# Layer 1 of a hybrid decoder: recurrence and output projection in one loop over blocks of 128 tokens

## The chip, the cores and the metric

The kernel runs on one core of a Trainium2 chip. The metric is the device time of one execution in microseconds, shown as the median of three runs. Beside it stands one execution with the hardware profiler on. Engines are named as the profile does: PE is TensorE's matrix unit and PEld its weight load, DVE is VectorE, ACT is ScalarE, POOL is GpSimd, SP issues most DMAs.

## The reference, cut to what matters

Two residual layers, 2048 tokens, width 1024, fp32. Layer 0 is a pooling and convolution mixer, layer 1 a gated DeltaNet with 8 heads of 128; each is followed by a mixture of experts. Layer 1's mixer is this:

```python
def gated_deltanet_mixer(h, w_in, conv_w, a_log, dt_bias, onorm_g, w_out):
    u = h @ w_in
    ...
    o = chunk_gated_delta_rule(l2norm(q), l2norm(k), v, beta, g)
    o = o * lax.rsqrt(jnp.mean(o * o, axis=-1, keepdims=True) + EPS) * onorm_g * jax.nn.silu(z)
    return o.reshape(bsz, seq, DN_WIDTH) @ w_out

# inside chunk_gated_delta_rule, for one chunk after the other:
def step(state, xs):
    qg_i, kd_i, u_i, w_i, a_i, d_i = xs
    v_new = u_i - jnp.einsum('bhck,bhkv->bhcv', w_i, state)
    o_i = jnp.einsum('bhck,bhkv->bhcv', qg_i, state) + jnp.einsum('bhcm,bhmv->bhcv', a_i, v_new)
    state = state * d_i[..., None, None] + jnp.einsum('bhck,bhcv->bhkv', kd_i, v_new)
    return state, o_i

# and around the mixer, in each layer:
    x = x + g_m * y
    hn = rmsnorm(x, norm_ffn[l]) * (1.0 + sc_f) + sh_f
    x = x + g_f * hierarchical_moe(hn, w_grp[l], b_grp[l], w_exp[l], b_exp[l], w_up[l], w_down[l])
```

What is left out of the mixer cuts u into q, k, v (after a short convolution and silu), z, beta and g.

## The kernel before

Layer 0 and its experts come first and are the same in both kernels. In layer 1, `dn_project` computes the projections of all tokens and stores what the recurrence needs to DRAM (`stg`, with A, KE, QG, KDD and VP for each block and head; `zT`; the diagonal blocks `ndia` for the inversion, and more).

`dn_chain` (from line 1320) then runs 16 blocks of 128 tokens in order, in two groups of four heads. `M(bl, hg)` assembles the block's inverse T out of 32x32 pieces: `spread` on POOL makes block-diagonal operands (`na`, `xo`, `tt`, line 1347), and six small steps alternate PE with DVE and ACT. `R(bl, hg)` is the recurrence: KE times the state S, `dv` on DVE (line 1454), T times dv (copied to `vt` by ACT), the output `po`, and the new state S (line 1472), for which POOL multiplies the old S by `etot` (`sd`, line 1459). `tail` makes the factor of the output norm (`ors` on POOL, `fac` on DVE) and scales the output on ACT; `O` transposes it on PE and multiplies it by onorm on DVE (line 1508) into a tile that is stored to `yT` in DRAM. The steps are generators, and the loop's body writes out by hand in which order their pieces are emitted; Tile's scheduler then gives each engine its own sequence, and an engine works through its sequence in order. Beside the first blocks, `dn_invert(1, 1)` inverts the diagonal blocks of the second half's second head group in 31 column steps on DVE (lines 1312 and 1313, tiles `xtmp` and `xblk`).

Then `out_phase(1, ...)` (from line 460) runs over the same 16 blocks. It loads w_out and splits it into a high and a low half (`woh`, `wol`; the helper `split`, lines 233 and 234, one on ACT, one on DVE); for each block it loads yT and zT, multiplies them (line 486), splits the product, and projects it with 48 matmuls of 128x512 (line 532: high by high, low by high, high by low). DVE multiplies the result by the gate row gm (line 536) and adds x (line 537); ACT takes the squares (line 540), `rstd` makes the norm's factor (`rs1t` on DVE, `rs` on POOL, lines 187 and 189), and DVE applies it and the shift (lines 542 and 543; in layer 0 line 543 is on POOL). The block goes to DRAM (`acc`, `hn`). `logits` transposes it and multiplies it by the routing weights, for two blocks at a time (line 567); `route` is called for groups of 4, 4, 4, 3 and 1 blocks, and `rank_experts` at the end. `moe(1)` follows.

## Time and profile before

| what | value |
| --- | --- |
| median of three runs | 3415.38 us (3412.9 to 3416.74) |
| the profiled execution, its own time | 3413.42 us |
| its span, from first to last instruction | 3411.7 us |
| PE busy | 2937.8 us, 86% |
| DVE busy | 2482.2 us, 73% |
| ACT busy | 1455.1 us, 43% |
| POOL busy | 1124.4 us, 33% |
| mean granted clock of PE | 0.927 |

The times of the profiled execution stand beside its own time, not beside the median. An engine's share is a mean over stages that have different limits, so the stages are read one by one. A wait is put down to the engine or DMA whose event came last. "Clock" is the share of full speed that the chip granted to PE in a stretch.

### The profile page before, as it was taken

Reading aid. Unit: us, or ns where it says so; the run is one execution under the profiler, and the core shown is the slowest. Engines: PE = TensorE matmul, PEld = TensorE weight load, DVE = VectorE, ACT = ScalarE, POOL = GpSimd, SP = SyncE. Lnnn points to the kernel's source line nnn. Section 1 sums busy time; section 2 is a strip of 40 time slices with the busy share of each in tenths; the row PEclk is TensorE's granted clock in tenths of the full one; section 3 lists DMA queues with packets and bytes.
Section 4 is the critical chain, followed back from the end, with each engine's and each line's share of the span. In section 5 each row is a group of like instructions: output and inputs, shape, how many; then the busy total and the mean of one; then the engine's idle time right before and its main releaser. Section 6 shows DMA issues by size and latency. Waiting matters only on the chain. (4 is left out here: it accounts for less than half of the span.)

```text
span 3411.7 us, 41792 instructions
## 1 busy us (share of the span) xinstructions
PE 2937.8 (86%) x14192; PEld 2345.7 (69%) x14192; DVE 2482.2 (73%) x3789; ACT 1455.1 (43%) x2430; POOL 1124.4 (33%) x913
## 2 busy tenths in 40 slices
PE   5979888769999969989888899887897996999991
PEld 3756666547777747777766777777896765777771
DVE  4998998748888856678867867856545556888883
ACT  6134223226565643333333233334663223656552
POOL 1143423333443413242323232235540122344341
PEclk9989989879999989999888999898998997999995
DMA  5216243729999852445442334347767535989875
GB/s 216 91 62 221 77 139 124 247 99 331 297 295 289 274 159 89 138 155 167 153 150 76 102 108 128 102 146 241 220 188 230 180 125 202 310 281 301 268 236 211
DMA packets 384987, 633.40 MB, mean 186 GB/s; under 512 B 111233, under 2 KB 245505, under 8 KB 384769
## 3 DMA queue, kind: packets, MB, share of 16 engines
q1 hardware_dynamic: 355904, 563.38, 48.7%
q0 software_dynamic: 28864, 67.30, 8.5%
q8 instruction: 114, 1.87, 0.2%
q14 instruction: 105, 0.85, 0.1%
HBM read 484.46 MB, written 175.44 MB: 193 GB/s over the span
## 5 line engine op out<-in xcount | busy, mean ns | idle before, releaser
L256 PE MATMUL pm<-hh,wh 128*128 128x512 f32 x1408 | 568.1, 404 | 0.9 <-ACT wh L233 0.7
L257 PE MATMUL pm<-hl,wh 128*128 128x512 f32 x1408 | 557.3, 396 | 4.1 <-DVE hl L229 4.1
L258 PE MATMUL pm<-hh,wl 128*128 128x512 f32 x1408 | 555.7, 395 | 4.3 <-DVE wl L234 4.3
L234 DVE TENSOR_TENSOR wl<-wr,wh 128x1024 fp32r<-128x1024 f32 x384 | 452.0, 1217 | 41.3 <-ACT wh L233 37.8
L233 ACT ACTIVATE wh<-wr 128x1024 fp32r<-128x1024 f32 x384 | 399.4, 1057 | 126.0 <-PE pu L815 57.5
L834 POOL DMA_INDIRECT acc<-ys,ixs x102 | 261.6, 2564 | 435.7 <-DVE wl L234 119.5
L256 PEld LDWEIGHTS pm<-hh,wh 128*128 128x128 f32 x1408 | 270.6, 192 | 63.2 <-issue 4.8
L257 PEld LDWEIGHTS pm<-hl,wh 128*128 128x128 f32 x1408 | 270.4, 192 | 63.4 <-DVE hl L229 4.5
L258 PEld LDWEIGHTS pm<-hh,wl 128*128 128x128 f32 x1408 | 268.8, 191 | 62.5 <-DVE wl L234 5.6
L813 PE MATMUL pu<-wh,xt 128*128 128x512 f32 x656 | 268.3, 409 | 0.5 <-ACT xt L233 0.5
L814 PE MATMUL pu<-wl,xt 128*128 128x512 f32 x656 | 261.1, 398 | 0.0
L815 PE MATMUL pu<-wh,xt 128*128 128x512 f32 x656 | 260.1, 397 | 0.0
L234 DVE TENSOR_TENSOR wl<-wraw,wh 128x1024 fp32r<-128x1024 f32 x88 | 126.3, 1435 | 171.9 <-ACT wh L233 171.7
L282 DVE SCALAR_TENSOR_TENSOR acc<-cin,wfir,acc 128x512 f32<-128x512 f32 (+1 forms) x320 | 214.5, 725 | 0.1
L532 PE MATMUL po<-woh,yh 128*128 128x512 f32 x512 | 172.9, 414 | 31.4 <-issue 11.6
L233 ACT ACTIVATE wh<-wraw 128x1024 fp32r<-128x1024 f32 x88 | 93.2, 1059 | 242.2 <-PE pm L257 242.0
L1210 DVE SCALAR_TENSOR_TENSOR dacc<-ub,cols,dacc 128x1024 f32<-128x1024 f32 x144 | 188.8, 1311 | 2.7
L532 PE MATMUL po<-wol,yh 128*128 128x512 f32 x512 | 166.7, 406 | 0.0
L532 PE MATMUL po<-woh,yl 128*128 128x512 f32 x512 | 165.8, 403 | 0.2 <-DVE yl L234 0.2
L791 POOL DMA_INDIRECT xg<-hn,ixs x102 | 111.3, 1091 | 165.8 <-PE tp L801 80.0
L189 POOL TENSOR_TENSOR rs<-rs1t,expo 128x1 f32<-128x1 f32 x48 | 28.3, 590 | 384.3 <-DVE rs1t L187 327.4
L815 PEld LDWEIGHTS pu<-wh,xt 128*128 128x128 f32 x656 | 123.8, 189 | 30.7 <-DVE xt L234 0.5
(378 smaller groups left out, 6511.3 us busy)
## 6 DMA issues: line engine op xcount, KB each, us to landing
wr<-in_w_up_dram SPq DMA_DIRECT2D x256, 512.0 KB, 7.5
wr<-in_w_down_dram SPq DMA_DIRECT2D x128, 512.0 KB, 7.2
modw<-in_modwT_dram SPq DMA_DIRECT2D x96, 512.0 KB, 5.0
wraw<-in_w_in_dram SPq DMA_DIRECT2D x88, 512.0 KB, 3.6
stin<-stg SPq DMA_DIRECT2D x32, 1280.0 KB, 8.9
yr<-yT SPq DMA_DIRECT2D x32, 512.0 KB, 4.6
acc<-xo SPq DMA_DIRECT2D x32, 512.0 KB, 4.0
hn<-ho SPq DMA_DIRECT2D x32, 512.0 KB, 3.2
```

The source lines that it names most:

```text
L233: a = nc.scalar.activation(h, x, AF.Copy) if eng == "act" else nc.vector.tensor_copy(h, x)
L234: return a, nc.vector.tensor_sub(l, x, h.bitcast(F32))
L256: nc.tensor.matmul(ps, wh[:, k], hh[:, k], start=k == 0, stop=False)
L257: nc.tensor.matmul(ps, wh[:, k], hl[:, k], start=False, stop=False)
L258: nc.tensor.matmul(ps, wl[:, k], hh[:, k], start=False, stop=k == KD - 1)
L282: self.tap = nc.vector.scalar_tensor_tensor(o, x, w, i, op0=ALU.mult, op1=ALU.add)
L532: nc.tensor.matmul(ps[:, ns], a[:, k], b[:, ns], start=k == 0 and i == 0, stop=k == KD - 1 and i == 2)
L813: nc.tensor.matmul(ps, xh[:, k], uh, start=k == 0, stop=False)
L814: nc.tensor.matmul(ps, xh[:, k], ul, start=False, stop=False)
L815: nc.tensor.matmul(ps, xl[:, k], uh, start=False, stop=k == KD - 1)
L834: st = nc.gpsimd.indirect_dma_start(out=self.acc, out_offset=bass.IndirectOffsetOnAxis(ap=ix[:, 0:1], axis=0), in_=ys, in_offset=None, bou ...
L1210: nc.vector.scalar_tensor_tensor(acc, ub[:, i:i + 1024], self.col("dn_conv", si * 4 + i), acc, op0=ALU.mult, op1=ALU.add)
```

## The change

`dn_chain` and the layer-1 use of `out_phase` are replaced by one function, `chain_out` (from line 1317 of the changed kernel), with one loop of 18 iterations. Iteration bl runs block bl of the recurrence, the projection of block bl - 2, the logits of block bl - 3 and, where a group is complete, pieces of the routing. `project` is a generator that gives away six matmuls at a time; `fill()` is called six times in an iteration and lets it, the routing and, in the first three iterations, the inversion and the preparation of w_out go on. The recurrence's output is multiplied by onorm and z where it leaves PE (line 1522), split, and stays in SBUF; yT is not stored to DRAM or loaded. The gate row gm is multiplied into w_out, once, on POOL, so that line 536 has no successor. The inversion `dn_invert(1, 1)` and the weights are completed at the end of iteration 2.

The memory for both phases now has to be there at once, and buffers are cut: the ring of PSUM banks `mm` from 4 to 2, `po` from 2 to 1, the projection's accumulator has one buffer, the inverse's operands (`wm`) 1 instead of 2, the loaded block inputs 3 instead of 5 and `stin` 4 instead of 6. `vt` and `dv` are written over KE and VP. The logits' matmuls take 128 columns each, not 256.

```diff
             cs = ep("cs", 1)
-            wm = ep("cwm", 2)
-            ld = ep("cld", 5)
+            wm = ep("cwm", 1)
+            ld = ep("cld", 3)
+            sp = ep("cst", NST)
             wk = ep("cwk", 2)
-            sp = [ep(f"cst{i}", 3) for i in range(2)]
-            zp = ep("cout", 2)
-            iv = ep("cinv", 1)
-            pm = ep("cpm", 4, space=PSUM)
+            wo = ep("cwo", 1)
+            ot = ep("cot", 1)
+            rt = ep("crt", 1)
+            pm = ep("cpm", 2, space=PSUM)
             pr = ep("cpr", 2, space=PSUM)
-            po_ = ep("cpo", 2, space=PSUM)
+            po_ = ep("cpo", 1, space=PSUM)
+            pp = ep("cpp", 1, space=PSUM)
+            pl_ = ep("cpl", 1, space=PSUM)
...
                 if bl:
-                    dv = t4(f"dv{hg}", 1)
-                    self.dv = nc.vector.tensor_sub(dv, VP, mm(KE, S, "pr", pr))
-                else:
-                    dv = VP
-                if 0 < bl < 15:
-                    sd = t4(f"sd{hg}", 1)
-                    nc.gpsimd.tensor_mul(sd, S, self.etot[:, hg * 4:hg * 4 + 4, bl:bl + 1].to_broadcast([P, 4, P]))
+                    nc.vector.tensor_sub(VP, VP, mm(KE, S, "pr", pr))
+                if bl < NT - 1:
+                    S2 = t4(f"S{hg}")
+                    if bl:
+                        nc.gpsimd.tensor_mul(S2, S, self.etot[:, hg * 4:hg * 4 + 4, bl:bl + 1].to_broadcast([P, 4, P]))
                 yield
-                vt = t4(f"vt{hg}")
-                self.vt = nc.scalar.activation(vt, mm(tt, dv, "pr", pr), AF.Copy)
+                vt = KE
+                nc.scalar.activation(vt, mm(tt, VP, "pr", pr), AF.Copy)
...
+            def load_z(t):
+                z = zs[t] = ot.tile([P, KD, P], F32, name="z")
+                half, o = divmod(t * P, 1024)
+                nc.sync.dma_start(z, self.zT[half][:, :, o:o + P].rearrange("k p t -> p k t"))
...
             def O(bl, hg):
-                on = outs.pop((bl, hg))
-                pt = pm.tile([P, 512], F32, name="mm")
+                on = pos.pop((bl, hg))
+                p = pm.tile([P, 512], F32, name="mm")
                 for h in range(4):
-                    nc.tensor.transpose(pt[:, h * P:(h + 1) * P], on[:, h], self.ident)
-                if hg == 0:
-                    done[bl] = zp.tile([P, 8, P], F32, name="ot", bufs=2)
-                nc.vector.tensor_scalar(done[bl][:, hg * 4:hg * 4 + 4], quad(pt), self.col("onorm"), None, op0=ALU.mult)
-
-            done = {}
-
-            def store(bl):
-                c, o = divmod(bl, 4)
-                nc.sync.dma_start(yT[c][:, :, o * P:(o + 1) * P].rearrange("h p t -> p h t"), done.pop(bl))
+                    nc.tensor.transpose(p[:, h * P:(h + 1) * P], on[:, h], self.ident)
+                z = zs[bl][:, hg * 4:hg * 4 + 4]
+                nc.vector.scalar_tensor_tensor(z, quad(p), self.col("onorm"), z, op0=ALU.mult, op1=ALU.mult)
...
+            def weights():
+
+                gm = ot.tile([P, D], F32, name="gm", tag="sh")
+                self.row_bcast(pm, self.mod[:, l * 48 + 16:l * 48 + 24], gm, "mm")
+                stage = []
+
+                def fetch(k):
+                    w = ot.tile([P, D], F32, name="wraw", tag=("z", "hT")[k % 2])
+                    nc.sync.dma_start(w, ins["w_out1"][k])
+                    stage.append(w)
+
+                fetch(0)
+                fetch(1)
+                yield
+                for k in range(KD):
+                    w = stage[k]
+                    nc.gpsimd.tensor_mul(w, w, gm)
+                    self.split(wh[:, k], wl[:, k], w)
+                    if k + 2 < KD:
+                        fetch(k + 2)
+                    yield
...
+            def project(t):
+
+                yh, yl = ysp.pop(t)
+                ps = pp.tile([P, D], F32, name="pp")
+                for k in range(KD):
+                    for i, (a, b) in enumerate(((yh, wh), (yh, wl), (yl, wh))):
+                        for n in range(2):
+                            ns = slice(n * 512, (n + 1) * 512)
+                            nc.tensor.matmul(ps[:, ns], a[:, k], b[:, k, ns], start=k == 0 and i == 0, stop=k == KD - 1 and i == 2)
+                    if k < KD - 1:
+                        yield
+                x = xs.pop(t)
+                nc.vector.tensor_add(x, ps, x)
+                nc.sync.dma_start(self.acc[t * P:(t + 1) * P], x)
+                h = hs[t] = ot.tile([P, D], F32, name="ho")
+                ss = self.small.tile([P, 1], F32, name="ss1")
+                nc.scalar.activation(h, x, AF.Square, accum_out=ss)
+                r = self.rstd(ss, 1.0 / D, 1, "rs1")
+                yield
+                nc.vector.scalar_tensor_tensor(h, x, r, cur["ga"], op0=ALU.mult, op1=ALU.mult)
+                nc.vector.tensor_add(h, h, cur["sh"])
+                nc.sync.dma_start(self.hn[t * P:(t + 1) * P], h)
...
+            def logits(t):
+                h = hs.pop(t)
+                t0, m = groups[t]
+                if t == t0:
+                    cur["pl"] = pl_.tile([P, 512], F32, name="pl")
+                pl, wr = cur["pl"], cur["wr"]
+                hT = ot.tile([P, KD, P], F32, name="hT")
+                for hf in range(2):
+                    p = pm.tile([P, 512], F32, name="mm")
+                    for j in range(4):
+                        k = hf * 4 + j
+                        nc.tensor.transpose(p[:, j * P:(j + 1) * P], h[:, k * P:(k + 1) * P], self.ident)
+                    nc.scalar.activation(hT[:, hf * 4:hf * 4 + 4], quad(p), AF.Copy)
+                    yield
+                o = (t - t0) * P
+                for k in range(KD):
+                    nc.tensor.matmul(pl[:36, o:o + P], wr[:, k], hT[:, k], start=k == 0, stop=k == KD - 1)
+                if t == t0 + m - 1:
+                    cur["route"] = self.route(l, t0, m, pl, mcum, rt, pm, "mm", ot, "hT")
...
+            inv = self.dn_invert(1, 1, ot, 2, ("xo", "ho"))
+            w = weights()
+            for bl in range(NT + 2):
+                chain = bl < NT
+                pj = project(bl - 2) if bl > 1 else iter(())
+                lg = logits(bl - 3) if bl > 2 else iter(())
+                rg = cur["route"]
+                t = tail(bl - 1) if 0 < bl <= NT else iter(())
+                if chain:
...
+                def fill():
+
+                    run(pj, rg, rg)
+                    if bl < 3:
+                        run(inv, inv)
+                        run(w)
+
+                run(t)
+                run(*r)
+                fill()
+                run(*m)
+                if bl + 3 < NT:
+                    load_n(bl + 3)
+                if 0 < bl <= NT:
+                    load_z(bl - 1)
+                run(lg)
+                run(r[0], m[0])
+                fill()
+                run(lg)
+                run(r[1], m[1])
+                run(t)
+                fill()
+                run(lg)
+                run(r[0], m[0])
+                if chain:
+                    load(*((bl + 2, 0) if NST > 3 else (bl + 1, 1)))
+                fill()
+                run(r[1], m[1])
+                if chain:
+                    load(*((bl + 2, 1) if NST > 3 else (bl + 2, 0)))
+                fill()
+                if 0 < bl <= NT:
+                    O(bl - 1, 0)
+                run(*m)
+                fill()
+                if 0 < bl <= NT:
+                    O(bl - 1, 1)
+                run(*nxt)
+                run(*m)
+                if bl == 2:
+                    all_of(inv)
+                    all_of(w)
+                if bl > 1:
+                    load_x(bl - 2)
+                all_of(pj)
+                all_of(rg)
+                if 0 < bl <= NT:
+                    split_y(bl - 1)
...
-        yT = [[T.dram.tile([KD, P, 512], F32, name=f"yT{l}_{c}") for c in range(NCH)] for l in range(2)]
-        T.layer0(yT[0])
+        yT = [T.dram.tile([KD, P, 512], F32, name=f"yT_{c}") for c in range(NCH)]
+        T.layer0(yT)
         T.moe(0)
-        T.mixer1(yT[1])
-        with tc.tile_pool(name="mraw1", bufs=RAW) as raw:
-            for _ in T.out_phase(1, yT[1], lambda t: T.x2[t * P:(t + 1) * P], None, raw):
-                pass
-            T.moe(1, raw)
+        T.mixer1()
+        T.moe(1)
```

How the sequences of the engines change is seen at three places. POOL, before, in one block of the steady recurrence: `sd` is S times etot, `ors` the output norm's power, and xo, tt and na are the spreads for a coming inverse.

```order
L1459 TENSOR_TENSOR sd_19968<-S_19865,etot 128x512
L1459 TENSOR_TENSOR sd_19977<-S_19898,etot 128x512
L189 TENSOR_TENSOR ors<-orst,expo 128x8
L1347 TENSOR_TENSOR xo_19983<-xh,m_18018 128x256
L1347 TENSOR_TENSOR xo_19991<-xh,m_18018 128x256
L1347 TENSOR_TENSOR tt_19985<-xd,m_18018 128x512
L1347 TENSOR_TENSOR tt_19993<-xd,m_18018 128x512
L1347 TENSOR_TENSOR na_19979<-no,m_18018 128x256
L1347 TENSOR_TENSOR na_19987<-no,m_18018 128x256
```

POOL now, at the same place of an iteration:

```order
L1465 TENSOR_TENSOR S_20934<-S_20661,etot 128x512
L1465 TENSOR_TENSOR S_20942<-S_20669,etot 128x512
L190 TENSOR_TENSOR ors<-orst,expo 128x8
L190 TENSOR_TENSOR rs_20912<-rs1t,expo 128x1
L1353 TENSOR_TENSOR na_21140<-no,m_18017 128x256
L1353 TENSOR_TENSOR na_21148<-no,m_18017 128x256
L1353 TENSOR_TENSOR tt_21146<-xd,m_18017 128x512
L1353 TENSOR_TENSOR tt_21154<-xd,m_18017 128x512
L1353 TENSOR_TENSOR xo_21144<-xh,m_18017 128x256
L1353 TENSOR_TENSOR xo_21152<-xh,m_18017 128x256
```

The projection's norm power `rs` has come in ahead of the spreads, and `na` stands first among them.

DVE now, from one iteration's end into the next; `fac` and `z` belong to the output of the recurrence, `xo`, `rs1t` and `ho` to the projection, `yl` to the split, and `stin` (line 1461) is what was `dv`:

```order
L188 TENSOR_SCALAR orst<-oss 128x8
L1498 TENSOR_TENSOR fac<-ors,fo 128x8
L1522 SCALAR_TENSOR_TENSOR z<-mm,cols,z 128x512
L1446 COPY w_18027<-mm 128x2x64
L1446 COPY w_18029<-mm 128x2x64
L1522 SCALAR_TENSOR_TENSOR z<-mm,cols,z 128x512
L1576 TENSOR_TENSOR xo<-pp,xo 128x1024
L235 TENSOR_TENSOR yl<-z,yh 128x1024
L1461 TENSOR_TENSOR stin<-stin,pr 128x4x128
L188 TENSOR_SCALAR rs1t<-ss_20908 128x1
L1461 TENSOR_TENSOR stin<-stin,pr 128x4x128
L1583 SCALAR_TENSOR_TENSOR ho<-xo,rs_20912,ga 128x1024
```

The `z` of the first head group stands behind `fac`; the residual addition, the split's low half and the first `dv` stand ahead of `rs1t`. And PE at the start of an iteration (pp is the projection, line 1424 the first product of the inverse, `pr<-stin,tt` the product of T and dv):

```order
L1376 MATMUL pr<-S_20661,stin 128x128 x4
L1376 MATMUL pr<-S_20669,stin 128x128 x4
L1572 MATMUL pp<-woh,yh 128x512 x2
L1572 MATMUL pp<-wol,yh 128x512 x2
L1572 MATMUL pp<-woh,yl 128x512 x2
L1424 MATMUL mm<-xt_20869,na_20867 128x32 x2
L1424 MATMUL mm<-xt_20877,na_20875 128x32 x2
L1376 MATMUL pr<-stin,tt_20600 128x128 x4
```

The inverse's first products now stand between six matmuls of the projection and the product with T.

The third place is DVE's end of the inversion. Before, the last steps stand ahead of block 5's `dv`:

```order
L1438 COPY w_18028<-mm 128x2x64
L1312 TENSOR_TENSOR xtmp<-xblk,nblk 128x31x31
L1438 COPY w_18030<-mm 128x2x64
L1313 TENSOR_REDUCE xblk<-xtmp 128x31
L1508 TENSOR_SCALAR ot<-mm,cols 128x512 x2
L1487 TENSOR_TENSOR oss<-oss,fo 128x8
L1454 TENSOR_TENSOR dv_19189<-stin,pr 128x512
L1488 TENSOR_TENSOR oss<-oss,fo 128x8
```

Now they stand ahead of block 2's state addition (line 1477):

```order
L1310 TENSOR_REDUCE xblk<-xtmp 128x30
L1309 TENSOR_TENSOR xtmp<-xblk,nblk 128x31x31
L1310 TENSOR_REDUCE xblk<-xtmp 128x31
L1477 TENSOR_TENSOR S_18654<-S_18654,pr 128x512
L1439 COPY x2t<-mm 128x128
L1477 TENSOR_TENSOR S_18662<-S_18662,pr 128x512
L1439 COPY x2t<-mm 128x128
```

The recurrence's block that the last step precedes has gone from the fifth to the second.

## Rows read from the trace of the kernel before

**Rows 1.** The page's head.

```profile
span 3411.7 us, 41792 instructions
```

**Rows 2.** Windows: stretch, us, busy (x count) per engine, granted clock, DMA share, GB/s.

```profile
2300.00:2420.00 120.00, 95.34 (x654) 87.60 (x652) 79.85 (x172) 56.14 (x212) 59.82 (x55) 0.84 0.69 207
2420.00:2560.00 140.00, 132.96 (x1139) 130.19 (x1139) 68.14 (x188) 95.80 (x358) 75.26 (x75) 1.00 0.72 221
2560.00:2590.00 30.00, 11.72 (x54) 8.78 (x53) 16.09 (x19) 18.62 (x43) 1.63 (x1) 0.64 0.86 280
2590.00:2820.00 230.00, 218.88 (x994) 166.06 (x993) 130.83 (x225) 51.61 (x83) 35.13 (x39) 0.96 0.52 165
```

**Rows 3.** Instructions of a tile and a line: ns min/median/max, first and last start.

```profile
L1454 DVE TENSOR_TENSOR dv<-stin,pr x20: 640/688/690, 2422.3 to 2555.5; 128x512 f32<-128x512 f32 x20
...
L532 PE MATMUL po<-woh,yh x256: 389/393/776, 2588.2 to 2826.1; 128*128 128x512 f32 x128
```

**Rows 4.** PE's waits: in 2420:2560, then 2560:2590; total us, times, longest.

```profile
PE mm L1442 <- DVE orst L187: 5.0, 8, 0.7
...
PE po L532 <- issue: 11.6, 1, 11.6
```

**Rows 5.** PE's timeline: start us, busy us, instructions (2500 and 2708 us).

```profile
2502.16 1.06 PE L1370 MATMUL pr<-vt,stin 128*128 128x128 f32 x8
2503.06 0.38 PE L1429 MATMUL mm<-ident,tl 128*128 128x128 f32 x2
2503.28 0.39 PE L1467 MATMUL po<-S,stin 128*128 128x128 f32 x2
...
2708.17 0.61 PE L532 MATMUL po<-woh,yh 128*128 128x512 f32 x2
...
2712.70 0.62 PE L532 MATMUL po<-wol,yh 128*128 128x512 f32 x2
```

**Rows 6.** Lines in 2590:2820: busy us, mean ns, idle before and its releaser.

```profile
L567 PE MATMUL rsm<-hT,wr 128*36 128x256 f32 x112 | 28.8, 416 | 0.4
...
L537 DVE TENSOR_TENSOR xo<-ho,xo 128x1024 f32<-128x1024 f32 x15 | 18.3, 1218 | 0.0
L234 DVE TENSOR_TENSOR yl<-yr,yh 128x1024 fp32r<-128x1024 f32 x15 | 18.2, 1216 | 1.1 <-ACT yh L233 1.1
...
L540 ACT ACTIVATE ho<-xo 128x1024 f32<-128x1024 f32 x15 | 15.9, 1058 | 26.7 <-DVE xo L537 26.7
...
L189 POOL TENSOR_TENSOR rs<-rs1t,expo 128x1 f32<-128x1 f32 x15 | 8.2, 548 | 171.7 <-DVE rs1t L187 171.7
...
L187 DVE TENSOR_SCALAR rs1t<-ss 128x1 f32<-128x1 f32 x15 | 2.3, 154 | 18.2 <-ACT ho L540 18.2
```

**Rows 7.** Lines in 2420:2560, the same columns.

```profile
L1459 POOL TENSOR_TENSOR sd<-S,etot 128x512 f32<-128x512 f32 x16 | 16.8, 1047 | 35.2 <-DVE S L1472 35.2
L189 POOL TENSOR_TENSOR ors<-orst,expo 128x8 f32<-128x8 f32 x10 | 16.3, 1634 | 15.5 <-DVE orst L187 14.5 <-DMA xh<-xinv 1.0
L1508 DVE TENSOR_SCALAR ot<-mm,cols 128x512 f32<-128x512 f32 x20 | 14.0, 736 | 0.0
...
L1472 DVE TENSOR_TENSOR S<-sd,pr 128x512 f32<-128x512 f32 x18 | 12.4, 687 | 20.6 <-PE pr L1370 20.0
...
L1347 POOL TENSOR_TENSOR na<-no,m 128x256 f32<-128x256 f32 x16 | 11.6, 742 | 0.0
...
L1493 DVE TENSOR_TENSOR fac<-ors,fo 128x8 f32<-128x8 f32 x10 | 2.6, 260 | 0.0
```

**Rows 8.** Windows for tile `xtmp` (busy, clock, DMA share, GB/s); DVE's timeline.

```profile
2340.00:2406.70 66.70, 44.15 (x62) 0.86 0.52 158
...
2406.69 0.67 DVE L1454 TENSOR_TENSOR dv<-stin,pr 128x512 f32<-128x512 f32 x1
```

**Rows 9.** Line 543, layer 0's instructions on POOL.

```profile
L543 POOL TENSOR_TENSOR ho<-ho,sh x16: 2337/2520/3479, 456.7 to 732.1; 128x1024 f32<-128x1024 f32 x16
```

**Rows 10.** PE's timeline, start of the recurrence; in brackets the idle time before.

```profile
2361.98 2.08 PE L1370 MATMUL pr<-dv,tt 128*128 128x128 f32 x8 [3.68 <-DVE dv L1454]
```

More of the change, by code (lines that the diff above doesn't have):

```diff
@@ L42 @@
 NYS = 3
+NST = 4
 def slots():
@@ L496, in out_phase @@
             wl = [p.tile([P, KD // 2, D], F32R, name="wol") for p in (wa, wb)]
[L497 to L503 removed]
+            both = wk.tile([P, 2, D], F32, name="wraw", tag="hT", bufs=1)
+            stage = [both[:, i] for i in range(2)]
+            stage += [wk.tile([P, D], F32, name="wraw", tag=t) for t in ("ho", "ho", "xo", "xo")]
+            stage += [cv.tile([P, D], F32, name="wraw", tag="acc", bufs=NACC) for _ in range(2)]
             for k in range(KD):
@@ L568, in logits @@
                 if t == t0 + m - 1:
-                    self.route(l, t0, m, pl, mcum, rt, pr)
+                    for _ in self.route(l, t0, m, pl, mcum, rt, pr):
+                        pass
             groups = {t: g for g in ((0, 4), (4, 4), (8, 4), (12, 3), (15, 1)) for t in range(g[0], g[0] + g[1])}
-            rest = iter(())
-            if l == 0:
-                rest = self.mod_rest(cv, [(0, i) for i in range(40, 48)] + [(1, i) for i in range(16)], tag="acc", bufs=NACC)
+            rest = self.mod_rest(cv, [(0, i) for i in range(40, 48)] + [(1, i) for i in range(16)], tag="acc", bufs=NACC)
             for t in range(NT):
@@ L1393, in load_n @@
                 for i in range(2):
-                    last = nc.sync.dma_start(nds[bl % 5][i * 64:(i + 1) * 64, :, i], self.stg[half][b][:64, i::2, 0, 64:])
+                    last = nc.sync.dma_start(nds[bl % 3][i * 64:(i + 1) * 64, :, i], self.stg[half][b][:64, i::2, 0, 64:])
                 blocks[bl] = (x, xd, no)
@@ L1444, in M @@
                 ready[bl, hg] = T
-            ready, outs, pos, oss = {}, {}, {}, {}
+            ready, pos, oss = {}, {}, {}
             def R(bl, hg):
@@ L1494, in tail @@
                 for hg in range(2):
-                    po = pos.pop((bl, hg))
-                    on = zp.tile([P, 4, P], F32, name=f"on{hg}", bufs=2)
+                    ob = pos[bl, hg]
                     for h in range(4):
-                        nc.scalar.activation(on[:, h], po[:, h], AF.Copy, scale=fac[:, hg, h:h + 1])
-                    outs[bl, hg] = on
+                        nc.scalar.activation(ob[:, h], ob[:, h], AF.Copy, scale=fac[:, hg, h:h + 1])
+            zs, ysp, xs, hs, cur = {}, {}, {}, {}, {}
@@ new lines, in chain_out @@
+            groups = {t: g for g in ((0, 4), (4, 4), (8, 4), (12, 3), (15, 1)) for t in range(g[0], g[0] + g[1])}
+            def logits(t):
[11 more added lines that the diff above has]
+                    nc.scalar.activation(hT[:, hf * 4:hf * 4 + 4], quad(p), AF.Copy)
+                    yield
+                o = (t - t0) * P
[3 more added lines that the diff above has]
+                    cur["route"] = self.route(l, t0, m, pl, mcum, rt, pm, "mm", ot, "hT")
@@ new lines, in all_of @@
+            def all_of(g):
+                for _ in g:
+                    pass
+            cur["route"] = iter(())
+            both = lambda bl: [load(bl, hg) for hg in range(2)]
+            with tc.high_priority(offset=400):
+                load_n(0)
+                both(0)
+                load_n(1)
+                if NST > 3:
+                    both(1)
+                else:
+                    load(1, 0)
+                last = load_n(2)
+            kg, zst, na, vp = self.stores[-4:]
@@ new lines, in behind @@
+            def behind(st, ld):
+                tc.add_manual_dep(st.ins, ld.ins.name,
+                                  mybir.DependencyInfo(mybir.DependencyClass.NoSync, mybir.DependencyReason.DATA),
+                                  reason="issued after the first loads")
+            for sd in (na, kg, zst, vp):
+                behind(sd, last)
+            g = [M(0, 0), M(0, 1)]
+            nxt = [M(1, 0), M(1, 1)]
+            run(*g)
+            for i in range(5):
+                run(*g)
+                if i == 1:
+                    run(*nxt)
@@ new lines, in chain_out @@
+            inv = self.dn_invert(1, 1, ot, 2, ("xo", "ho"))
[7 more added lines that the diff above has]
+                if chain:
+                    r = [R(bl, 0), R(bl, 1)]
+                    m, nxt = nxt, [M(bl + 2, hg) if bl < NT - 2 else iter(()) for hg in range(2)]
+                    oss[bl] = self.small.tile([P, 2, 4], F32, name="oss")
+                else:
+                    r = m = [iter(())] * 2
+                    nxt = m
+                def fill():
[33 more added lines that the diff above has]
+                    O(bl - 1, 1)
+                run(*nxt)
+                run(*m)
[8 more added lines that the diff above has]
+                    split_y(bl - 1)
@@ L1595, in pack @@
+            all_of(cur["route"])
+            all_of(logits(NT - 1))
+            all_of(cur["route"])
+            self.rank_experts(1, mcum[:, NT % 8], rt, pm, "mm")
 def pack(inputs):
```

197 lines of the change are left out of this document (72 added, 125 removed).

## The prediction

> **What bounds the kernel now.** The span is 3411.7 us [rows 1]; I read its stretches around the change first. Layer 1 from the recurrence to the projection has four of them [rows 2]: a start (2300 to 2420 us) with TensorE (PE) busy 95 of 120 us at a clock of 0.84; a steady recurrence (2420 to 2560) with PE busy 133 of 140 at full clock; a seam (2560 to 2590) with PE busy 12 of 30; and the projection phase (2590 to 2820) with PE busy 219 of 230. So both long stretches already stand at 95% of PE's time, and only the start and the seam have room. Then the pace: the subtraction `dv` comes twice a block, 20 times from 2422.3 to 2555.5 us, so a block of the recurrence takes 133.2 / 9 = 14.8 us; the projection's matmuls run from 2588.2 us to the four behind the last listed start, 2826.1, so to some 2827.2, for 16 blocks: 14.9 us a block [rows 3]. One block of each costs 29.7 us, say 29.8 with the seam's side effects left out. That is the number that an iteration of the new loop has to beat.
>
> Then the waits. In the steady recurrence PE waits for others some 7 us in 140, the largest group 5.0 us in eight waits; in the seam it stands 11.6 us before the first projection matmul [rows 4]. The reader should see that the seam is worth some 20 us, once (30 us with PE busy for 12), and that inside the two loops hardly anything is idle for the other to fill.
>
> **The change, part by part.** *Removed.* The store and load of yT (16 blocks of 512 KB each way) were beside other work: the cover is PE's 219 busy us of 230 [rows 2], so I price them at nothing; without that cover they could cost at most the 11 us that are left. The gm multiplication (1.22 us, VectorE, DVE) goes from each block, but DVE was busy 131 of 230 us there [rows 2], so this too is nothing on the path; without the cover it would be 1.22 us a block. The seam goes: minus some 20 us.
>
> *PE's work in a merged iteration.* The recurrence: 133 of 140 us busy, so 14.05 us of a 14.8 us block [rows 2]. The projection: 20 matmuls of 512 columns took 2712.70 - 2708.17 = 4.53 us, 0.2265 us each, and 48 make 10.87 us. The transposes of the normalised block: 8 records, at the recurrence's 0.90 us for 8 [rows 5]. The logits: 28.8 us busy for 14 blocks, 2.06 us [rows 6]. Sum 27.9 us. If nothing were ever waited for, this would be the iteration, 2 us below the 29.8.
>
> *First new wait: `na` behind the norm's `rs`.* GpSimd (POOL) works in order, and in the new program the power for the projection's norm (`rs`, line 190) stands ahead of the spreads `na`, on which the first product of the next block inverse (line 1424) waits. In before `na` was the end of a POOL sequence that waited for no such thing. Count from the last projection matmul of a block, t = 0. DVE, in its order: the residual addition, 1.22 us; the low half `yl`, 1.22; one `dv`, 0.69 [rows 3]; then the small op `rs1t`, 0.15. ScalarE's (ACT) square, 1.06 us after the addition, is done before that. So `rs1t` ends at 3.3 us; `rs` takes 0.55 and the two `na` 0.74 each [rows 6, 7], and four hand-overs between engines cost some 0.3 (an estimate). The first `na` is ready at 4.9, the second at 5.6. PE meanwhile has two state products (16 records, 0.90 us for 8 [rows 5], 1.8 us) and six projection matmuls (1.36): it arrives at 3.2 us. Both inverse products stand next to each other in PE's order, so all the rest of the recurrence and projection queues behind them: PE loses some 2.2 us (5.6 less 3.2, less 0.2 of work between). Lower bound 0, if the norm's chain is over by 3.2 us because the additions start earlier than the last matmul's modelled end; upper bound 3, if POOL is late itself. I take 2.2, since every step is a row.
>
> *Second new wait: `z` behind `fac`.* The output's transposes now take a bank of a ring of two (it was four), and the bank is freed by the DVE operation on `z` (line 1522). In DVE's order that stands behind `fac`, which waits for POOL's `ors`, which stands behind the two products S times etot. From the end of the second `po` group: state product 0.90 [rows 5], S addition 0.69, POOL's product 1.05, `ors` 1.63, `fac` 0.26 and `z`, by the nearest operation 0.74 [rows 7]; with the hand-overs (0.3, as above) the bank is free at 5.5 us. PE has the state product, two transposes (0.22), six projection matmuls (1.36), the output's four transposes (0.45), an inverse product (0.2) and four projection matmuls (0.9), and arrives at 4.0 us at a product that needs that bank: 1.5 us lost. In the iterations with a routing piece (one in four) DVE has `z` ahead of `fac` and this wait falls away; that is inside the rounding. Bounds: 0 and 2. In before PE waited in this tail for 5.0 us in eight waits (line 1442, behind the small DVE operations), at most 0.7 each [rows 4]; that is with four banks.
>
> [...]
>
> So an iteration: 27.9 + 2.2 + 1.5 = 31.6 us, less some 0.1 for the iterations without the second wait averaged in with what the routing adds: **31.5 us**, against 29.8 for the two it replaces.
>
> *The start.* The last inversion step of half 1 (31 steps, 62 DVE instructions, 44.15 us busy, lines 1312 and 1313) was spread in before over three blocks and ended just ahead of the `dv` of block 5 at 2406.69 [rows 8]. Now it must end within iteration 2: in DVE's order the state addition of block 2 stands behind the last step. DVE has there 44.15 us of it, eight weight splits (8 x 1.22 = 9.8, by the same shape [rows 6]) and some 12 us of the recurrence: 66 us. In before it lay whole behind 2340 us [rows 8]; now its start has no block of the recurrence ahead, and I let it begin between 2333 and 2349 us. Then the last step ends between 2399 and 2415, and the next block's `dv`, some 6 to 8 us later, stands between 2405 and 2423. I take **2413 us** for the start of iteration 3, where before stood half a block into block 5. The multiplication of w_out by gm on POOL (its nearest row, an addition of the same shape, 2.52 us [rows 9]; eight are 20 us) lies beside the inversion; if that cover were gone, it would be late by less than these 20.
>
> *The end.* Iterations 3 to 14 are whole. Iteration 15 has no block inverse and no state update, 48 of a block's 120 matmul records: 14.05 - 5.6 + 13.8 + one wait of 1.5 = 23.7. Iterations 16 and 17 are a projection block with its logits (13.8) and waits for single buffers, 2.5 to 3 us by the two chains above: 16.6 and 16.2. Sum 56.5. From the last projection matmul on, the routing, the ranking and the gathers are as before; the weights of the experts were not loaded before the ranking in before either, so the hand-over stays: 0.
>
> **Sum.** 2413 + 12 x 31.5 + 56.5 = 2847.5 us for the end of the last projection matmul, against 2827.2: plus 20 us. The profiled execution took 3413.4 us (1.7 around the span), 2 us under the median of the runs, 3415.4. On the median's scale that is 3435 us, slower by 0.6%.
>
> **Rivals.**
> - *The loop runs at PE's bound.* If both waits vanish (the order hides them, or the durations are shorter without contention), an iteration costs 27.9 to 28.5: 2413 + 12 x 28.2 + 55 = 2806, minus 21: 3394 us, faster. For it: PE is the bound in both stretches [rows 2]; the projection matmuls need nothing of the same iteration, and should fill every gap. Against it: the fill is in PE's order, and cannot pass a waiting product. It decides where an iteration is under 29.8 us: when of the 3.7 us of waits less than 2 remain.
> - *A wash.* One of the two waits falls away, 29.8 to 30 us an iteration: 3410 to 3422 us.
> - *The waits bring down the clock.* In before a wait of 3.68 us is followed by matmuls at half the speed: eight records took 2.08 instead of 1.06 us [rows 5, 10], a granted clock in that stretch of 0.84 against 1.00 in the steady one [rows 2]. If two waits in each iteration did that, with 2 to 3 us lost, an iteration would be 34 us and the time 3465. Against it: waits of 0.7 us kept 1.00, and the waits here are of 1.5 and 2.2. [...]
> - *The change does less than it says at the start*: should the inversion not gate iteration 2, iteration 3 starts at about 2400, 13 us earlier, in any of the cases.
>
> **How the numbers follow.** The forecast 0.48, the loop at PE's bound 0.23, a wash 0.15, the clock 0.14. A measurement of this kernel tells some 0.2%, 7 us, from no change. Faster 0.23, same 0.17, slower 0.60. The range goes from 3398, just above the first rival (a part of its chance lies above that), to 3466 at the last one; its likeliest case alone spans 3422 to 3448, from an iteration 1 us shorter and a start 10 us late or early.
>
> **What would show it.** In the profile after: whole iterations of 31 us, the `dv` of line 1461 as their mark; PE's waits with line 1424 behind POOL's `na` at some 2 us an iteration, and line 1445 behind DVE at some 1.5; a start of iteration 3 near 2413; a granted clock of 1.00 in the steady stretch; no wait for z, x or the stored inputs. I am wrong if iterations take under 29.8 us, if the two waits are not in the list, if the clock falls below 0.95 there, or if DVE's inversion ends 20 us from 2407.

## The result: slower by 1.0%, and where the time went

The changed kernel took 3449.25 us (median of 4 runs, 3442.12 to 3452.26), before 3415.65; the ratio is 1.0097, with an interval of 1.0079 to 1.0114. The forecast was 3435 us, slower. The profiled execution has a span of 3450.6 us, 38.9 more than [rows 1].

The first view is again the pace: the last projection matmuls against [rows 3], whose last `woh,yh` started at 2826.1 us. Columns: ns min/median/max, first and last start.

```profile
L1572 PE MATMUL pp<-woh,yh x256: 386/398/793, 2395.8 to 2870.0; 128*128 128x512 f32 x128
```

The projection ends 43.9 us later than before; the part behind it gives 5 back. The `dv` of block 3, which marks iteration 3, came at 2423.66 us (forecast 2413), that of block 15 at 2808.3: twelve iterations of 32.05 us on the mean (forecast 31.5). Three of them, and the whole stretch, in the windows view (the columns of [rows 2]):

```profile
2423.66:2453.72 30.06, 28.42 (x193) 24.80 (x192) 13.80 (x27) 14.28 (x45) 11.57 (x10) 1.00 0.63 195
2453.72:2485.14 31.42, 29.84 (x193) 26.18 (x192) 13.49 (x26) 14.16 (x45) 11.54 (x10) 0.95 0.54 166
...
2546.90:2585.82 38.92, 31.77 (x205) 27.52 (x204) 22.57 (x67) 15.76 (x48) 19.05 (x18) 0.87 0.44 134
...
2423.70:2808.30 384.60, 354.23 (x2329) 309.09 (x2328) 180.35 (x379) 174.49 (x526) 144.31 (x128) 0.96 0.49 153
```

Three kinds of iteration are to be seen. Five take 30.1 us or a little less at a clock of 1.00, with PE busy for 28.4; five take 31.4 to 31.7 with the same 193 matmul records, but at a clock of 0.95 and with PE busy for 30.0; two, those in which the routing's results are scattered, take 38.9 and 37.7. PE's waits name the causes (total us, times, longest): first 2424 to 2809 us, then the start from 2300, then the end from 2809.

```profile
PE mm L1445 <- DVE z L1522: 15.5, 10, 1.6
PE mm L1450 <- DVE w L1446: 14.3, 2, 7.2
...
PE mm L1437 <- ACT sh L201: 22.4, 1, 22.4
PE mm L1424 <- ACT gm L201: 14.2, 1, 14.2
...
PE pp L1572 <- ACT yh L234: 8.6, 1, 8.6
```

The wait for `z` is there, at 1.6 us for a forecast of 1.5. The wait for `na` is not in the list at all. In its place stand two waits of 7.2 us for the copy `w` and one of 8.6 for `yh`, which were not forecast.

**The wait for z.** DVE's timeline in one iteration (start us, us):

```profile
2605.44 0.17 DVE L188 TENSOR_SCALAR orst<-oss 128x8 f32<-128x8 f32 x1
2607.37 0.17 DVE L1498 TENSOR_TENSOR fac<-ors,fo 128x8 f32<-128x8 f32 x1 [1.76 <-POOL ors L190]
2607.46 0.74 DVE L1522 SCALAR_TENSOR_TENSOR z<-mm,cols,z 128x512 f32<-128x512 f32 x1
2608.12 0.28 DVE L1446 COPY w<-mm 128x128 f32<-128x128 f32 x1
```

PE beside it, and then the same projection matmuls in an iteration of the first kind:

```profile
2608.26 0.66 PE L1445 MATMUL mm<-x2t,nd 128*128 128x64 f32 x4 [1.58 <-DVE z L1522]
...
2610.35 1.20 PE L1572 MATMUL pp<-woh,yh 128*128 128x512 f32 x2
2611.35 0.63 PE L1572 MATMUL pp<-wol,yh 128*128 128x512 f32 x1
```

```profile
2509.41 0.70 PE L1572 MATMUL pp<-woh,yh 128*128 128x512 f32 x2
2509.95 0.40 PE L1572 MATMUL pp<-wol,yh 128*128 128x512 f32 x1
```

`fac` waits 1.76 us for POOL, `z` starts 0.09 us behind it, and PE goes on when z is done. After the wait two projection matmuls took 1.00 us to the next start, where they take 0.54: PE ran at half its clock, for some 3 us by the granted clock of 0.95 over 31.7 us; from 2609.80 to 2613.00 us it was granted 0.50. It did so in five of the ten iterations with this wait, each time after 1.58 us.

**The wait that was not there.** POOL and PE at the start of an iteration:

```profile
2618.31 0.55 POOL L190 TENSOR_TENSOR rs<-rs1t,expo 128x1 f32<-128x1 f32 x1 [10.97 <-DVE rs1t L188]
2618.85 2.41 POOL L1353 TENSOR_TENSOR na<-no,m 128x256 f32<-128x256 f32 x2
```

```profile
2618.19 0.97 PE L1424 MATMUL mm<-xt,na 128*128 128x32 f32 x8
```

POOL's order is as forecast, `na` behind `rs`; but PE's first inverse product starts ahead of that `na`. It reads the one that was made an iteration earlier: the spreads are a block ahead. The listings ahead of the prediction show it too: in the iteration that reads `S_20661`, POOL writes `na_21140` and PE reads `na_20867`.

**The long iterations.** POOL, DVE and PE in one of them:

```profile
2564.08 1.10 POOL L704 DMA_INDIRECT lst<-pay,sl  x1 [1.11 <-DVE sl L702]
...
2573.07 0.96 POOL L704 DMA_INDIRECT lst<-pay,sl  x1 [0.30 <-issue]
2574.05 1.70 POOL L190 TENSOR_TENSOR ors<-orst,expo 128x8 f32<-128x8 f32 x1
```

```profile
2575.78 1.02 DVE L1498 TENSOR_TENSOR fac<-ors,fo 128x8 f32<-128x8 f32 x1 [7.62 <-POOL ors L190]
2576.72 0.28 DVE L1446 COPY w<-mm 128x128 f32<-128x128 f32 x1
```

```profile
2577.05 1.22 PE L1450 MATMUL mm<-xe,w 128*128 128x128 f32 x4 [7.15 <-DVE w L1446]
```

Eight scatters take POOL 10 us to issue, `ors` stands behind them, `fac` behind `ors`, and one of the two copies `w` behind `fac`.

**The start.** The inversion's last step began at 2409.25 us (forecast: its end at 2399 to 2415). Two rows of DVE show the same instruction at two times, and POOL beside the first:

```profile
2364.97 2.30 DVE L1498 TENSOR_TENSOR fac<-ors,fo 128x8 f32<-128x8 f32 x1 [1.54 <-POOL ors L190]
...
2415.12 0.17 DVE L1498 TENSOR_TENSOR fac<-ors,fo 128x8 f32<-128x8 f32 x1 [1.75 <-POOL ors L190]
```

```profile
2364.90 2.34 POOL L1549 TENSOR_TENSOR wraw<-wraw,gm 128x1024 f32<-128x1024 f32 x1
```

`fac` reads 128x8 elements and takes 0.17 us; beside a multiplication of w_out by gm it took 2.30 us and ended with it.

PE's wait for `sh` has to do with the same multiplications. The row `sh` takes the buffer of `gm` (the tag "sh" in the code), so it can be copied out of PSUM only behind the last of the eight. POOL, ACT and PE:

```profile
2373.35 5.84 POOL L1549 TENSOR_TENSOR wraw<-wraw,gm 128x1024 f32<-128x1024 f32 x2 [6.11 <-DMA wraw<-in_w_out_dram]
2380.19 1.06 ACT L201 ACTIVATE sh<-mm 128x512 f32<-128x512 f32 x2
2380.82 0.69 PE L1437 MATMUL mm<-ident,tl 128*128 128x128 f32 x2 [22.43 <-ACT sh L201]
```

### The profile page after: what moved, and what is told of

The parts are those of the page before. It is cut to its first block, busy times and chain, and to the rows that moved or that the text cites. A ratio compares the mean times of both kernels' runs of the same rounds, so it can differ in the third digit from the quotient of the medians.

```text
span 3450.6 us, 41921 instructions
## 1 busy us (share of the span) xinstructions
PE 2938.1 (85%) x14304; PEld 2354.9 (68%) x14304; DVE 2483.3 (72%) x3757; ACT 1467.2 (43%) x2428; POOL 1160.3 (34%) x921
## 5 line engine op out<-in xcount | busy, mean ns | idle before, releaser
L190 POOL TENSOR_TENSOR rs<-rs1t,expo 128x1 f32<-128x1 f32 x48 | 28.2, 588 | 362.9 <-DVE rs1t L188 292.1
L812 PEld LDWEIGHTS pu<-wh,xt 128*128 128x128 f32 x656 | 123.9, 189 | 30.6 <-DVE xt L235 0.5
L810 PEld LDWEIGHTS pu<-wh,xt 128*128 128x128 f32 x656 | 124.2, 189 | 28.9 <-ACT xt L234 1.6
L811 PEld LDWEIGHTS pu<-wl,xt 128*128 128x128 f32 x656 | 124.5, 190 | 26.3
L845 DVE SCALAR_TENSOR_TENSOR ys<-py,ixs,gf 128x512 f32<-128x512 f32 x164 | 118.6, 745 | 31.6 <-PE py L844 31.6
```

The costliest lines, as they stand in the source:

```text
L810: nc.tensor.matmul(ps, xh[:, k], uh, start=k == 0, stop=False)
L811: nc.tensor.matmul(ps, xh[:, k], ul, start=False, stop=False)
L812: nc.tensor.matmul(ps, xl[:, k], uh, start=False, stop=k == KD - 1)
L845: nc.vector.scalar_tensor_tensor(ys[:, ns], PY[n], ix.bitcast(F32)[:, 2:3], gf[:, ns], op0=ALU.mult, op1=ALU.mult)
```

## The experiments

My theory A was: the loop's waits come from DVE's order (`z` and `w` behind `fac`), the extra length of the long iterations from the scatters ahead of `ors`. Theory C: at the start DVE is the bound, held up by POOL's multiplications. The rivals: two PSUM banks are too few in any order (B), and the start is bound by PE's two long waits (E). "Iteration 3" below is the first `dv` of block 3; means are over iterations 3 to 14. The runs are compared by their ratios to before.

**1. fac behind z** (`issue_after` orders DVE alone):

```diff
-                nc.vector.tensor_mul(fl(fac), r, fl(fo))
+                with tc.issue_after(zlast[-1]) if zlast else ExitStack():
+                    nc.vector.tensor_mul(fl(fac), r, fl(fo))
...
+                zlast.append(zi.ins)
```

> Changed kernel (3449 us) with one order forced: DVE's fac of a block stands behind the last z of the block before, not ahead of it. Theory A (the order on DVE is the new wait: z, and in the iterations with the scatters the copy w, stand behind fac, which waits for POOL): PE's waits for z (10 of 1.6 us) and for w (2 of 7.2 us) vanish, the clock stays at 1.00, an iteration takes 28.5 to 29 us instead of 32.05 on the mean, and the 8.6 us wait in iteration 16 goes too: 3449 - 12 x 3.3 - 8, some 3400 us (3395 to 3410). Rival B (two banks for mm are too few, whatever the order): the wait moves to the next user of a bank (line 1445 or 1450) and keeps most of its size: 3430 to 3445 us.

Measured: 3420.62 us, ratio 1.0024 (1.0014 to 1.0034), 25 us less than 1.0097. The windows of a usual and of a long iteration, and of one behind a long one:

```profile
2475.00:2503.20 28.20, 28.15 (x193) 24.84 (x192) 13.69 (x26) 14.12 (x44) 11.58 (x10) 1.00 0.62 185
2531.50:2565.90 34.40, 29.57 (x205) 25.60 (x204) 22.68 (x66) 15.45 (x47) 19.07 (x18) 0.98 0.53 165
...
2686.10:2718.30 32.20, 32.20 (x195) 28.50 (x193) 12.36 (x27) 14.12 (x45) 10.58 (x10) 0.87 0.41 135
```

A usual iteration is PE's work and nothing else, 28.2 us, at a clock of 1.00. The waits for z and w are gone; B is refuted as a rule for every order. But two iterations still take 34.4 us: there PE waits 4.8 us for `yh`, which on ACT stands behind the scaling by `fac`. The iterations behind them take 29.3 and 32.1 us; PE is busy in them from end to end, at a clock of 0.96 and 0.87. And in iteration 16 a wait of 7.7 us for `yh` is left of the 8.6. I had counted on these going too, and so the gain was smaller than forecast.

**2. The scatters behind ors**, all eight in one piece (a dependency of order alone, from each scatter to the `ors` of the same iteration; `fac` still ahead of z).

> Changed kernel with the routing's eight scatters on POOL (10 us of issue) forced behind the output norm's power ors of the same iteration; fac still ahead of z. Theory A: the two long iterations (38.9 and 37.7 us) fall to 31 or 32, and the 8.6 us wait of iteration 16 goes, the other iterations keep 30 and 31.6: 3449 - 2 x 6.5 - 7, some 3429 us (3424 to 3436). Rival (the scatters' issue only moves and now holds back rs, then ho and the inverse's w behind it): 3442 to 3449 us.

Measured: 3448.0 us, ratio 1.0090 (1.0069 to 1.0112). The rival was right, as POOL and PE's waits in the iteration behind show:

```profile
2579.63 0.95 POOL L711 DMA_INDIRECT lst<-pay,sl  x1 [0.30 <-issue]
2580.61 0.59 POOL L191 TENSOR_TENSOR rs<-rs1t,expo 128x1 f32<-128x1 f32 x1
```

```profile
PE mm L1609 <- DVE w L1434: 3.9, 1, 3.9
```

The iteration with the scatters fell from 38.9 to 30.9 us, the next rose from 31.7 to 36.7: now `rs`, and `ho` and `w` behind it, wait for the last scatter.

**3. Without the multiplication by gm** (the line `nc.gpsimd.tensor_mul(w, w, gm)` left out). The routing then sees other values and sends other tokens to the experts, so the whole time, 3561.89 us, says nothing; only the start is read.

> Changed kernel without the eight multiplications of w_out by the gate row gm on POOL: this part of the computation is left out, the row is still made. Theory C (DVE is the bound of iterations 0 to 2, and is held up while POOL multiplies: DVE instructions that start beside one end with it): the inversion's last step comes 10 to 15 us earlier than 2410.4, the time is 3434 to 3440 us. Rival D (the multiplications lie beside the inversion, whose 44 us and the splits are the bound): within 3 us of 3449.

**4. The rows gm, ga and sh in the projection's PSUM tile**:

```diff
-                self.row_bcast(pm, self.mod[:, l * 48 + 16:l * 48 + 24], gm, "mm")
+                self.row_bcast(pp, self.mod[:, l * 48 + 16:l * 48 + 24], gm, "pp")
...
```

> Changed kernel with the three broadcast rows gm, ga and sh made in the projection's own PSUM tile, not in the ring mm. Theory C (DVE bounds the start): PE's waits of 14.2 us (for gm) and 22.4 us (for sh) vanish, but the inversion's last step stays within 4 us of 2410.4 and the time within 4 us of 3449. Rival E (the start is PE's: its stalls behind the two banks delay the blocks): iteration 3 starts 15 to 25 us earlier, 3425 to 3434 us.

The inversion's last step in 3, then in 4 (in the changed kernel 2409.25):

```profile
2390.79 1.16 DVE L1310 TENSOR_REDUCE xblk<-xtmp 128x31 f32<-128x961 f32 x1
```

```profile
2394.77 1.14 DVE L1311 TENSOR_REDUCE xblk<-xtmp 128x31 f32<-128x961 f32 x1
```

Without the multiplications the last step came 18.5 us earlier and iteration 3 started at 2406.4, 17.3 us earlier: more than theory C said, and far from its rival. But this run takes away two things at once: `sh` was copied at 2343.9 us, and PE did not wait for it.

With the rows elsewhere and the multiplications in place the last step came 14.5 us earlier and iteration 3 started at 2411.6, 12 us earlier (3438.14 us, ratio 1.0073, 1.0056 to 1.0090). Here theory C was wrong and E nearer, though short of its 15 to 25 us. Of the two waits that were to vanish only that for `gm` fell, from 14.2 to 4.2 us; that for `sh` stayed, at 24.8. DVE from the inversion's first step to its last, in the changed kernel and then in 4 (busy times of PE, PEld, DVE, ACT and POOL behind the length):

```profile
2327.06:2409.25 82.19, 45.48 (x245) 41.38 (x246) 73.18 (x100) 28.11 (x72) 39.06 (x22) 0.65 0.44 129
```

```profile
2325.51:2394.77 69.26, 22.92 (x117) 19.65 (x117) 66.63 (x80) 18.60 (x34) 33.38 (x19) 0.57 0.48 141
```

DVE is idle for 9.0 of 82.2 us and for 2.6 of 69.3, so it is nearly the bound in both. PE's waits add to that, and in 4 twenty fewer of DVE's instructions lie in the stretch. How the 12 us divide was not tried.

**5. gm in the loop**, as in before, in a buffer of its own; `stin`, the block inputs of the text below, has 3 buffers, not 4, which makes room for the row:

```diff
-                nc.vector.tensor_add(x, ps, x)
+                nc.vector.tensor_mul(h, ps, cur["gm"])
+                nc.vector.tensor_add(x, h, x)
...
```

> Changed kernel (3449 us; 3444 on the scale of the last runs) with gm not multiplied into w_out on POOL but, as in before, into the projected block on DVE (one 128x1024 instruction more in each iteration); for the 4 KB that the row takes, the block inputs have 3 buffers, not 4. Theory C (POOL's multiplications hold up DVE at the start, and DVE has 14 of 30 us idle in an iteration): iteration 3 starts some 17 us earlier, iterations stay at 30.1 and 31.7: 3424 to 3432 us. Rival (DVE's addition of 1.2 us is on the path to rs, ho and dv, or the third buffer is missed): the start's gain is given back, 1 to 1.5 us an iteration, 3440 to 3450 us.

Measured: 3433.05 us, ratio 1.0054 (1.0037 to 1.0071). Iteration 3 at 2400.0, 23.7 us earlier; usual iterations 30.5 and 32.05, each 0.4 longer: nearer theory C (3424 to 3432 us), with a small price in the loop that I had put at nothing. The start gained more than the 17 us of the forecast; here too PE's wait for `sh` is gone, and that for `gm` is 10.1 us.

**6. fac behind z and the scatters in two halves**: four behind `ors`, four behind the spreads of the next iteration.

> fac behind z as before it, and the routing's scatters on POOL in two halves: four behind ors, four behind the spreads of the next iteration. Theory A (the four long iterations left, 34.5, 34.4, 32.1 and 29.3 us, are the scatters ahead of ors or rs): all whole iterations 28.0 to 28.8 us, some 3404 us, a ratio to before of 0.995 to 0.999. Rival (the scatters' 10 us of issue fit nowhere on POOL): a wait moves to another place, the ratio stays at 1.000 to 1.003.

Measured: 3397.58 us, ratio 0.9953 (0.9937 to 0.9970). The twelve iterations in one window:

```profile
2418.80:2758.80 340.00, 339.39 (x2329) 299.12 (x2328) 178.39 (x379) 173.12 (x526) 144.56 (x128) 1.00 0.56 174
```

PE is busy for 339.4 of 340.0 us, 28.3 us an iteration, no long ones left. The merged loop is faster than before once two things in its order are changed.

**7 to 9. All together**, with the rows in the projection's tile: gm in the loop (7), on DVE into w_out (8), on POOL into w_out (9).

> All together: fac behind z, the scatters in halves, the rows in the projection's PSUM tile, gm in the loop on DVE (3 buffers for the block inputs). If the effects add up: e6 less 17 to 25 us at the start: 3380 to 3388 us, a ratio of 0.989 to 0.992. If the start has another bound below (the block inputs' DMAs, DVE's inversion): less 8 to 12 us, 3392 to 3396.

> As the run with all, but gm multiplied into w_out on DVE (eight instructions of 1.22 us) instead of in the loop, with 4 buffers. Theory C (the price on POOL is the time in which DVE stands still, some 18.7 us; on DVE it is 9.8): iteration 3 starts 10 us later than in the run with gm in the loop: 3390 to 3398 us. Rival (the multiplications' engine does not matter at the start): within 3 us of the run with gm in the loop.

> As the run with gm multiplied into w_out on DVE, but on POOL again: fac behind z, scatters in halves, rows in the projection's PSUM tile. Theory C (POOL's eight multiplications stop DVE for their 2.34 us each, 18.7 us, against 9.8 on DVE): iteration 3 starts 7 to 10 us later than 2407.5, a ratio of 0.9945 to 0.9955. Rival (the engine does not matter, the three rows and the order were what the start cost): within 3 us of 2407.5, 0.991 to 0.993.

| run | us | ratio (interval) | iteration 3 at | mean of iterations 3 to 14 |
| --- | --- | --- | --- | --- |
| 7, gm in the loop | 3384.64 | 0.9916 (0.9899 to 0.9932) | 2398.8 | 28.83 |
| 8, gm on DVE | 3387.70 | 0.9924 (0.9908 to 0.9941) | 2407.5 | 28.44 |
| 9, gm on POOL | 3389.81 | 0.9938 (0.9921 to 0.9955) | 2410.8 | 28.33 |

The effects added up as forecast for 7, which beats both kernels: 0.84% below before. Of 8 against 7, iteration 3 came 8.7 us later (forecast 10), of which the shorter iterations give back 4.7; its time fell below its forecast, and the two ratios cannot be told apart. 9 against 8 is not what theory C said: 3.3 us later, not 7 to 10, and these ratios cannot be told apart either. The inversion on DVE, 2300 to 2420 us, in run 8 and then in run 9 (busy us, mean ns, idle before):

```profile
L1322 DVE TENSOR_TENSOR xtmp<-xblk,nblk 128x1 f32<-128x1 f32 (+30 forms) x31 | 26.9, 868 | 2.7 <-POOL xblk L1316 2.1
L1323 DVE TENSOR_REDUCE xblk<-xtmp 128x1 f32<-128x1 f32 (+30 forms) x31 | 15.5, 500 | 0.7
```

```profile
L1322 DVE TENSOR_TENSOR xtmp<-xblk,nblk 128x1 f32<-128x1 f32 (+30 forms) x31 | 37.1, 1197 | 2.8 <-POOL xblk L1316 2.1
L1323 DVE TENSOR_REDUCE xblk<-xtmp 128x1 f32<-128x1 f32 (+30 forms) x31 | 15.6, 502 | 0.8
```

Beside POOL's multiplications the 31 instructions with two SBUF inputs take 10.2 us longer, the 31 with one input no longer. In run 8 DVE is spared that and does the multiplications itself, 9.8 us: the last step starts at 2395.4 in run 8 and at 2395.7 in run 9. So theory C was right that DVE's instructions take longer beside POOL's multiplications, but its price of 18.7 us was too high; the two prices are nearly equal, and the engine hardly matters. Run 7's lead of 8.7 us at the start goes with the eight multiplications, on either engine, and with PE's wait for `sh` (18.6 us in run 8, 24.7 in run 9, none in run 7). A run with a buffer of its own for gm and the multiplication into w_out, which would tell these apart, was not made.

**10. The kernel before with the two cuts in PSUM alone** (`cpm` from 4 to 2 banks, `cpo` from 2 to 1).

> The kernel before with the two cuts in PSUM of the change alone: the ring mm from 4 banks to 2, po from 2 to 1. Theory A (two banks are enough where six projection matmuls lie between their uses; without these they are not): blocks of the recurrence take 16.5 to 18 us in place of 14.8, 30 to 50 us in all. Rival (two banks are enough in any case): within 7 us of before.

Measured: 3430.61 us (two runs), ratio 1.0055 (1.0033 to 1.0076), 19 us; a block of the steady recurrence takes 15.5 us on the mean of eight, not 14.8. Neither theory had the size (16.5 to 18 us a block, or within 7 us of before in all). PE's largest wait there, from 2425 to 2570 us, is not for `mm`:

```profile
PE po L1467 <- ACT ob L1477: 7.0, 9, 0.9
```

It is for the single `po`, which in the merged loop never shows. So in these blocks the fill between two uses of a bank can be worth 0.7 us, less than I had said. The rest of the 19 us lies elsewhere; the block ahead of the eight took 20.4 us.

**11. z's transposes in the ring pr**, with DVE's order as it was:

```diff
-                p = pm.tile([P, 512], F32, name="mm")
+                p = pr.tile([P, 512], F32, name="pr")
```

> Changed kernel (a ratio of 1.010 to before) with its order unchanged, but the output's transposes in the other PSUM ring, pr, so that z, late behind fac, holds no bank of mm. Theory A (PE waits only because late z holds one of two banks): the ten waits of 1.6 us vanish and the clock stays at 1.00, as in the run with fac behind z; of the two long iterations some 6 us remain: a ratio of 1.001 to 1.004. Rival (DVE's order costs PE whatever bank z holds, by the copies w behind fac): the waits stay at 1 us or more, 1.006 to 1.010.

Measured: 3422.05 us, ratio 1.0037 (1.0023 to 1.0052); usual iterations 28.9 us at a clock of 1.00. PE's waits from 2417 to 2780 us:

```profile
PE pr L1376 <- DVE z L1522: 6.1, 2, 3.1
PE mm L1450 <- DVE w L1446: 4.1, 10, 0.4
```

So it is the pair that costs: a late z, and the bank that it holds. Either remedy takes the wait away; the copies `w`, late too, cost 0.4 us each.

## Why the prediction was right, and which of its steps were not

The direction, the range and the reason at its core (an order in which late work holds what PE needs) stood. Of its own signs of being wrong one came true by half: of the two waits one is not in the list. The size came out as +20 us forecast, +34 measured, 38.9 between the two profiled executions. These 38.9 are the forecast with four errors: start +10.7, twelve iterations +6.6, end +6.3, behind the projection -5.0. Part by part:

- *PE's work in an iteration*, 27.9: measured 28.2 (run 1). Right; so was the break-even of 29.8.
- *First new wait, na behind rs, 2.2 us*: the step failed. The order on POOL was read rightly, but not which block's `na` it is. The buffer numbers in the listings would have shown it. It cost nothing. That the mean iteration of 32.05 us came near 31.5 all the same is luck: in place of these 2.2 us stand 1.2 us of waits for `w` (14.3 us over twelve iterations) and 1.2 us of clock (below).
- *Second new wait, z behind fac, 1.5 us*: right, 1.58, and shown by runs 1 and 11 from two sides. Its four hand-overs, put at 0.3 us without a row, are in size too: from the end of `z` at 2608.20 to PE at 2608.26 it is 0.06, from the end of `S` on DVE at 2603.99 to POOL at 2604.13 it is 0.14. That two banks would bring the full wait, and not the 0.7 us of four banks, was not shown by a row; it came, but with fac behind z the same two banks cost nothing (run 1), so the number of banks is not the cause by itself.
- *"In the iterations with a routing piece this wait falls away; that is inside the rounding"*: this is the step that failed worst. In these iterations the issue of eight scatters on POOL, 10 us, stands ahead of `ors`. The two took 38.9 and 37.7 us, some 15 us above the others together, and a third set of scatters, from 2822.3 us on, stands ahead of the wait of 8.6 us in iteration 16. Runs 2 and 6 show this cause: with the scatters moved that wait is 2.1 and 2.8 us. I had not counted them.
- *The clock*: I had made it a rival of its own at 34 us an iteration. It came in part: 1.6 us in five usual iterations, 8 us in all, and the rest in the long ones. In the twelve iterations PE was busy for 354.2 us, in run 6 for 339.4 with the same 2329 records. With the waits gone the clock is 1.00 in the usual iterations of run 1 and throughout in run 6.
- *The start*, 2413: it was 2423.7. The step that failed is DVE's 66 us of work up to the last step: 83 us lay between the inversion's start at 2327.1, 6 us before the earliest that I allowed, and its end at 2410.4. In it gm on POOL, "beside the inversion", stood at nothing, with a bound of 20 us if that cover were gone; leaving it out is worth 17 us at the start (run 3), by DVE's longer instructions and by the wait for `sh` together. The rows that wait in the ring `mm` were not in the sum either; moving them is worth 12 us (run 4). The next `dv` came 13.3 us behind the last step, not 6 to 8. That the sum came out only 11 us off is luck: the early start of the inversion hid a part.
- *The end*: 2808.3 to 2871.1 for iterations 15 to 17 (1.1 us behind the last start, as in the prediction), 62.8 us, against 56.5: in the main the wait of 8.6 us. Behind the projection 5 us came back (forecast 0); the cause of that was not tried.

The likeliest case was thus right in kind. The rival "the loop runs at PE's bound", 3394 us, is what the same loop does with another order: 3398 us in run 6.

## What to carry to other kernels

Two loops that each keep PE at 95% have at best the seam and their few per cent to gain from merging; here that was 30 us, and it came only when the order and the start were mended. In a merged loop, list for every in-order engine what now stands ahead of what, issues of DMAs too, and ask of each operand which iteration made it; a wait read off one engine's order alone can be a block away from the truth. When an operation that frees a bank stands behind one that waits for a slow engine, either its place in the order or its bank can be changed: here that gave 25 us (run 1) and 20 us (run 11), which cannot be told apart, and the order of the scatters as much again (run 6). And when two tiles share a buffer, ask what the second now waits for: `sh` waited for the last use of `gm`.

## What the hardware showed that I had not expected

While POOL multiplied 128x1024 elements in SBUF (2.34 us), a DVE operation of two SBUF inputs that started beside it did not end before it: 2.30 us for a `fac` of 0.17 us. In the inversion the 31 instructions with two SBUF inputs took 26.9 us without these multiplications on POOL and 37.1 beside them, the 31 with one input 15.5 and 15.6 (runs 8 and 9). What holds the one engine up beside the other is not shown.

A wait of 1.58 us was followed by half the clock in five iterations (0.69 granted over the 5.5 us from its end), and by full clock, 1.00, in five others of the same work (four with 1.58 or 1.59 us, one with 1.32). What tells them apart stays open.
